# Feature tiles of the input projection: three 256-column matmuls per weight tile, or one of 512 columns and one of 256

## The chip, the cores and the metric

The kernel runs on one core of a Trainium2 chip. The metric is the device time of one execution in microseconds (us), the median of several runs. The core has five engines that matter here: TensorE (PE in the profile, with its weight loads as PEld), VectorE (DVE), ScalarE (ACT), GpSimd (POOL) and the DMA queues of SyncE (SP). Each engine works off its own instructions in the order in which they stand in the program, and waits at an instruction until what it needs is there.

## The reference

Two layers of a decoder trunk on 256 tokens with 1024 features, in float32. What is changed is the product `h @ w_in`.

```python
for l in range(DEPTH):                       # two layers
    h = rms_norm(x, norm_mix[l])
    z = h @ w_in[l]                          # 1024 x 4768, the input projection
    c_q, c_kv, k_pe, hq, hf, hi, hg, g_a, g_b = jnp.split(z, offsets, axis=-1)
    y_a = mla_mixer(c_q, c_kv, k_pe, ...) @ w_proj_a[l]        # latent attention
    y_b = hgrn2_mixer(hq, hf, hi, hg, ...) @ w_proj_b[l]       # gated recurrence
    y = sigmoid(g_a) * y_a + sigmoid(g_b) * y_b
    x = x + y @ w_out[l]
    h = rms_norm(x, norm_ffn[l])
    x = x + (silu(h @ w_gate[l]) * (h @ w_up[l])) @ w_down[l]
```

## The kernel before

**Two parts for every operand.** Each float32 operand of a large product is split into a high part and a remainder, both in the float32r format of TensorE. ScalarE writes the high part of a weight chunk (`wh`, L113), VectorE the remainder (`wl`, L115). For half of each of the chunks t3 to t6 GpSimd writes the remainder in its place (`ON_POOL`). A product is then the sum of three: high by high, high by remainder, remainder by high. `mm3` (L191) issues these three as matmuls of 256 columns (the 256 tokens), each with its own weight load. `mmw` (L205) exists too, and the two SwiGLU products use it: because the two parts of the activations lie side by side in `xx` as [8, 2, 256], one matmul of 512 columns takes both with the high weights, and a second of 256 columns adds the remainder of the weights to the first half of the PSUM bank. The bank's halves must then be added on the way out.

**Chunks and tiles.** 33 blocks of 128 output features ("tiles" below) of the input projection are computed with features on partitions and tokens as columns. `T_CHUNKS` puts one into chunk t0 and two into each of t1 to t16, and `tchunk(ci)` computes a chunk: both tiles into the two halves of one PSUM bank, eight weight tiles of 128 features deep, 24 matmuls per tile. Then one VectorE instruction per chunk (L277 or L281) multiplies the whole bank, 512 columns, by the norm's scale `rb` on its way to SBUF; for t9 to t16 a ScalarE tanh follows (L282). t0 to t2 give the attention's latents, t3 and t4 the forget gates `hf`, t5 and t6 the recurrence's queries `hq`, t7 and t8 its output gate, t9 to t16 the merge gates.

**PSUM.** The pool `acc` has two banks, for t0, t1 and t3 to t16 (t2 takes one of `hgp`) and for the two token tiles of the recurrence's values (`hia`, L313). A chunk can begin when the chunk but one before it has been read out of its bank.

**Order.** The Python code issues t0 to t2, the latents, the keys and queries of attention (L365 to L404), then t3 to t16 with steps of attention (`next(at)`) and of the recurrence (`next(rec)`) between chunks, so that TensorE has matmuls of the projection while the other engines work at softmax and recurrence. A list scheduler of the framework then sets the final order on each engine. Weights are prefetched up to two chunks ahead into five buffers for `wh` and five for `wl`, each of half a chunk, so one tile uses one buffer of each. `gates(h)` (L495 to L500) takes `hf` through exp (ScalarE), an addition (GpSimd), a reciprocal and two scalings (VectorE); `rows` (L600, L601) and `products` (L540) begin the recurrence once `hq` and the gates are there.

Of the kernel before, what the change touches and what calls it, by code (L numbers as in the profile page):

```python
# [9 lines left out]
F32 = mybir.dt.float32  # L10
# [4 lines left out]
ALU = mybir.AluOpType  # L15
# [17 lines left out]
# columns of the packed per-partition vectors  # L33
# [3 lines left out]
# weight parts whose remainders GpSimd takes, where the vector engine has most to do  # L37
# [6 lines left out]
def chunk_plan():  # L44
    """Chunks of one layer in the order of their use: (name, columns per partition)."""
    plan = [("t0", 1024)]
    plan += [(f"t{i}", 2048) for i in range(1, 3)]
    plan += [("hib", 2176), ("ukv", 2048), ("uq0", 1152), ("uq1", 1152)]
    plan += [(f"t{i}", 2048) for i in range(3, 7)]
    plan += [("hia", 2176)]  # L50
    plan += [(f"t{i}", 2048) for i in range(7, 17)]
    plan += [(f"proj{i}", 2048) for i in range(4)]
    plan += [(f"out{i}", 2048) for i in range(4)]
    plan += [(f"gu{i}", 2048) for i in range(KF)]
    plan += [(f"dn{i}", 2048) for i in range(11)]
    return plan
# [10 lines left out]
# the 33 feature tiles of w_in that are computed with features on partitions  # L67
# [12 lines left out]
def trunk(ctx: ExitStack, tc: tile.TileContext, x_in, w_in, vec_in, gqk_in, cst_in, msk_in, out):  # L80
# [44 lines left out]
    # intra-tile score matrices of the recurrence (transposed); entries above the causal  # L125
    # diagonal stay zero
# [32 lines left out]
    # lower bounds of the forget gates: lbm = 1 - lb per layer  # L159
# [22 lines left out]
    def split(hi, lo, src, scale=None):  # L182
        """hi + lo = src * scale, both parts float32r."""
        if scale is None:
            S.copy(hi, src)
            V.tensor_tensor(lo, src, hi.bitcast(F32), ALU.subtract)
        else:
            S.activation(hi, src, AF.Copy if isinstance(scale, float) else AF.Identity, scale=scale)  # L188
            V.scalar_tensor_tensor(lo, src, scale, hi.bitcast(F32), ALU.mult, ALU.subtract)  # L189
# [15 lines left out]
    def mmw(ps, items):  # L205
        """Both parts of the moving operand in one pass; ps[:, 0] + ps[:, 1] is the product."""
        n = len(items)
        for i, ((ah, al), b) in enumerate(items):
            PE.matmul(ps, ah, b, start=i == 0, stop=False)  # L209
            PE.matmul(ps[:, 0], al, b[:, 0], start=False, stop=i == n - 1)  # L210

    def token_stats(src, kt, both=False):
        """Sum of squares over features (partitions and kt tiles) per token -> PSUM [tok, TT]."""
        tot = None
        for k in range(kt):
            sq = wk.tile([P, T], F32, tag="w1", bufs=3, name="sq")
            if k % 2 or not both:
                S.activation(sq, src[:, k], AF.Square)  # L218
            else:
                V.tensor_tensor(sq, src[:, k], src[:, k], ALU.mult)  # L220
            if tot is None:
                tot = sq
            else:
                G.tensor_tensor(tot, tot, sq, ALU.add)  # L224
        ps = trp.tile([P, 512], F32, name="trp")
        for t in range(TT):
            PE.matmul(ps[:, t:t + 1], tot[:, t * P:(t + 1) * P], ones[:, 0:1], start=True, stop=True)
        return ps[:, 0:TT]

    def norm_in(l, col):  # L230
        """Split gain * x, and the norm's scale per token, [tok, TT] and broadcast over partitions."""
# [18 lines left out]
    for l in range(L):  # L250
# [11 lines left out]
        def tchunk(ci):  # L262
            W = weights(l, f"t{ci}")
            tiles = T_CHUNKS[ci]
            if ci == 2:
                ps = hgp.tile([P, 2, T], F32, name="hgp")
            else:
                ps = acc.tile([P, 2, T], F32, name="acc")
            for j in range(len(tiles)):
                o = j * KD * P  # L270
                mm3(ps[:, j], [(W(o + k * P, P), xs[k]) for k in range(KD)], late=l == 0 and ci == 0)
            n = len(tiles)
            a = tiles[0]
            rbb = bc(rb.unsqueeze(1), [P, n, T])
            for lo, hi, dst in ((0, 5, cq), (5, 9, hf), (9, 13, hq), (13, 17, sg)):
                if lo <= a < hi:
                    V.tensor_tensor(dst[:, a - lo:a - lo + n], ps[:, :n], rbb, ALU.mult)  # L277
            if a >= 17:
                m = (a - 17) // 2
                g = wk.tile([P, 2, T], F32, name="gs", bufs=2)  # L280
                V.tensor_tensor(g, ps, rbb, ALU.mult)  # L281
                S.activation(gab[:, m], g, AF.Tanh, scale=0.5)  # L282
# [4 lines left out]
        # latents: gain and split; their norms' scales come in after the next product  # L287
# [33 lines left out]
        # rotary tables with the gains; the gains of the other dimensions go to the queries  # L321
# [33 lines left out]
        def heads_T(dst, src, t, i):  # L355
            """Four heads of 128 tokens, their dimensions to partitions."""
# [63 lines left out]
        # scale of each row of scores  # L420
# [9 lines left out]
        # causal softmax and its product with the values  # L430
# [60 lines left out]
        # gates: k = (1 - lb) sigmoid(-hf), f = 1 - k  # L491
# [10 lines left out]
        # Scores by the highest bit in which two positions differ. Level h: row t (bit h set)  # L502
        # against column s in the first half of the same 2h block. q carries the decay since its
        # h block's start, k the decay to its h block's end, tot the blocks' whole decays. One set
        # of k serves levels h and 2h: for 2h, columns of the block's first h block also need the
        # decay of the second, which all rows of the second half share.
# [24 lines left out]
        def tiles(ap, h, u):  # L531
            """One head's positions with bit h set to u: [tile, block, position]."""
            return half(ap, h, u).rearrange("p (t n) c -> p t n c", t=TT)

        def products(rw, cols):
            """Scores of one head's columns k against the packed rows."""
# [15 lines left out]
        def blocks(h):  # L552
            """Levels whose columns are whole groups of 32 partitions."""
# [41 lines left out]
        def recurrence():  # L595
            # the diagonal and level 1
# [14 lines left out]
            # levels 2 and 4, levels 8 and 16  # L611
# [135 lines left out]
def _tiles(w, ks, ms):  # L747
    """[K, M] -> [128, ms, ks, 128]: the weight tiles of each output tile side by side."""
# [3 lines left out]
def _pack(inp):  # L752
# [36 lines left out]
    # constants of the shapes  # L789
# [37 lines left out]
```

## Time and profile before

| | us |
|---|---|
| median of 3 runs (787.41 to 787.87) | 787.68 |
| span of the profiled execution, first to last instruction | 785.7 |
| between the two (what lies around the span) | 2.0 |
| PE busy | 769.1 (98%) |
| PEld busy | 716.8 (91%) |
| DVE busy | 614.7 (78%) |
| ACT busy | 414.8 (53%) |
| POOL busy | 277.7 (35%) |

The busy time of PE is not a measure of how fast its matmuls follow each other: they are pipelined, and a matmul's row lasts longer than the distance to the next. That distance is read from the starts in the timeline. A plain float32 matmul (transposes, scores, the recurrence) stands as two records in the trace in most lines. The shares over the whole span mix stages: the input projection with attention and recurrence lies at 20 to 167 us in the first layer and 400 to 551 us in the second, the SwiGLU behind each.

### The profile page before, as it was taken

How to read it: one execution, taken by the hardware profiler on the slowest of the kernel's cores; microseconds unless marked ns; L12 is line 12 of the kernel's file. 1: busy time of each engine (PE TensorE's matmuls, PEld its weight loads, DVE VectorE, ACT ScalarE, POOL GpSimd, SP SyncE). 2: the span in 40 equal slices, each digit the busy share in tenths (PEclk: the TensorE clock that was granted, in tenths of full speed). 3: DMA queues.
4: the chain of work that ended last, by engine and by line, in shares of the span. 5: the costliest groups of instructions: out<-in, count | busy, mean ns of one | idle time of the engine just before them, and what ended most of it. 6: DMA issues, size and time to landing. Idle time of an engine off the chain costs nothing.

```text
span 785.7 us, 13803 instructions
## 1 busy us (share of the span) xinstructions
PE 769.1 (98%) x5376; PEld 716.8 (91%) x5376; DVE 614.7 (78%) x958; ACT 414.8 (53%) x744; POOL 277.7 (35%) x296
## 2 busy tenths in 40 slices
PE   5999999999999999999999999999999999999998
PEld 4999999999988888888899999999999888888887
DVE  7799986658979888886668898856687988888652
ACT  5665754444655656554447557444354655655430
POOL 5696422003234343421037823311223334444000
PEclk9999999999999999999999999999999999999999
DMA  7743334425554545455534443334454564545630
GB/s 244 261 166 126 143 112 158 161 108 216 172 204 161 210 166 212 166 211 205 193 122 161 165 161 108 137 134 161 161 181 149 208 214 168 209 168 208 226 131 20
DMA packets 20658, 133.27 MB, mean 170 GB/s; under 512 B 2417, under 2 KB 3569, under 8 KB 5361
## 3 DMA queue, kind: packets, MB, share of 16 engines
q1 hardware_dynamic: 20592, 132.39, 47.3%
q8 instruction: 42, 0.69, 0.3%
q14 instruction: 24, 0.19, 0.1%
HBM read 131.33 MB, written 1.05 MB: 168 GB/s over the span
## 4 chain that ended last, share of the span: by engine, by line
PE 82%; DVE 12%; issue 3%; POOL 1%; ACT 1%; DMA 1%; SPq 0%; DVEq 0%; POOLq 0%; ACTq 0%
PE acc L209 15%; PE acc L210 8%; PE acc L202 8%; PE acc L203 8%; PE acc L201 8%; PE prj L209 5%; PE hgp L209 5%; PE trp L209 5%; DVE wl L115 3%; PE trp L210 3%; PE hgp L210 3%; PE prj L210 3%; PE hgp L540 2%; DVE hf L498 1%; PE prj L201 1%
## 5 line engine op out<-in xcount | busy, mean ns | idle before, releaser
L115 DVE TENSOR_TENSOR wl<-st,wh 128x1024 fp32r<-128x1024 f32 (+3 forms) x241 | 327.1, 1359 | 68.2 <-ACT wh L113 67.3
L113 ACT CAST wh<-st 128x1024 fp32r<-128x1024 f32 (+2 forms) x250 | 257.8, 1035 | 178.3 <-PE acc L202 88.5
L201 PE MATMUL acc<-xx,wh 128*128 128x256 f32 x488 | 141.1, 289 | 0.0
L203 PE MATMUL acc<-xx,wl 128*128 128x256 f32 x488 | 139.2, 286 | 0.0
L202 PE MATMUL acc<-xx,wh 128*128 128x256 f32 x488 | 139.0, 285 | 0.0
L209 PE MATMUL acc<-ff,wh 128*128 128x512 f32 x352 | 122.4, 391 | 0.0
L210 PE MATMUL acc<-ff,wl 128*128 128x256 f32 x352 | 98.9, 282 | 0.0
L202 PEld LDWEIGHTS acc<-xx,wh 128*128 128x128 f32 x488 | 93.3, 191 | 0.3
L201 PEld LDWEIGHTS acc<-xx,wh 128*128 128x128 f32 x488 | 93.3, 191 | 0.3
L203 PEld LDWEIGHTS acc<-xx,wl 128*128 128x128 f32 x488 | 93.2, 191 | 0.1
L722 POOL TENSOR_TENSOR g<-g,rb 128x256 f32<-128x256 f32 x44 | 37.2, 846 | 135.3 <-DVE g L721 123.0
L209 PEld LDWEIGHTS acc<-ff,wh 128*128 128x128 f32 x352 | 66.1, 188 | 14.2 <-DVE ff L189 0.4
L727 POOL TENSOR_TENSOR hd<-th,g 128x256 f32<-128x256 f32 x44 | 66.1, 1503 | 7.4 <-DVE th L725 4.5
L188 ACT ACTIVATE ff<-hd 128x256 fp32r<-128x256 f32 x44 | 18.4, 418 | 94.4 <-POOL hd L727 94.4
L224 POOL TENSOR_TENSOR sq<-sq 128x256 f32<-128x256 f32 x34 | 33.9, 996 | 96.7 <-ACT sq L218 58.8
L210 PEld LDWEIGHTS acc<-ff,wl 128*128 128x128 f32 x352 | 66.5, 189 | 0.1
L209 PE MATMUL prj<-xx,wh 128*128 128x512 f32 x176 | 62.4, 396 | 0.0
L209 PE MATMUL acc<-xx,wh 128*128 128x512 f32 x176 | 62.3, 394 | 0.0
L209 PE MATMUL hgp<-xx,wh 128*128 128x512 f32 x176 | 62.1, 394 | 0.0
L209 PE MATMUL trp<-xx,wh 128*128 128x512 f32 x176 | 62.0, 393 | 0.0
L210 PE MATMUL acc<-xx,wl 128*128 128x256 f32 x176 | 49.0, 279 | 0.0
L210 PE MATMUL hgp<-xx,wl 128*128 128x256 f32 x176 | 48.8, 277 | 0.0
(238 smaller groups left out, 1765.4 us busy)
## 6 DMA issues: line engine op xcount, KB each, us to landing
st<-in_w_dram SPq DMA_DIRECT2D x115, 1024.0 KB, 4.7
st<-in_w_dram SPq DMA_DIRECT2D x4, 1088.0 KB, 4.9
st<-in_w_dram SPq DMA_DIRECT2D x4, 576.0 KB, 3.5
st<-in_w_dram SPq DMA_DIRECT2D x4, 512.0 KB, 5.1
xT<-in_x_dram SPq DMA_DIRECT2D x4, 256.0 KB, 4.8
out_dram<-xT SPq DMA_DIRECT2D x8, 128.0 KB, 1.9
mst<-in_msk_dram SPq DMA_DIRECT2D x1, 288.0 KB, 7.2
cst<-in_cst_dram SPq DMA_DIRECT2D x1, 260.0 KB, 7.4
```

Of the source, the lines that this page charges most:

```text
L113: S.copy(wh[:, :n_], st[:, c:c + n_])
L115: eng.tensor_tensor(wl[:, :n_], st[:, c:c + n_], wh[:, :n_].bitcast(F32), ALU.subtract)
L188: S.activation(hi, src, AF.Copy if isinstance(scale, float) else AF.Identity, scale=scale)
L201: PE.matmul(ps, ah, bh, start=i == 0, stop=False)
L202: PE.matmul(ps, ah, bl, start=False, stop=False)
L203: PE.matmul(ps, al, bh, start=False, stop=i == n - 1)
L209: PE.matmul(ps, ah, b, start=i == 0, stop=False)
L210: PE.matmul(ps[:, 0], al, b[:, 0], start=False, stop=i == n - 1)
L224: G.tensor_tensor(tot, tot, sq, ALU.add)
L540: PE.matmul(ps[:, t * 192:(t + 1) * 192], kk[:, hd, t * P:(t + 1) * P], rt[:, t], start=True, stop=True)
L722: (V, G)[j].tensor_tensor(g[:, j], g[:, j], rb, ALU.mult)
L727: G.tensor_tensor(hd, th, g[:, 1], ALU.mult)
```

## The change

From t3 on each tile gets a bank of `acc` of its own and is computed with `mmw`: eight pairs of a 512-column and a 256-column matmul in place of 24 of 256 columns. Per tile, ScalarE copies the bank's second half to `g`, and VectorE adds the first half to it. Per chunk, GpSimd multiplies both tiles by `rb` into the destination, where VectorE did it out of PSUM before. t0 to t2 are left as they were. The rest of the change is comments that are taken out; the lines of the changed kernel that follow `tchunk` stand ten lines lower.

```diff
         def tchunk(ci):
             W = weights(l, f"t{ci}")
             tiles = T_CHUNKS[ci]
-            if ci == 2:
-                ps = hgp.tile([P, 2, T], F32, name="hgp")
-            else:
-                ps = acc.tile([P, 2, T], F32, name="acc")
-            for j in range(len(tiles)):
-                o = j * KD * P
-                mm3(ps[:, j], [(W(o + k * P, P), xs[k]) for k in range(KD)], late=l == 0 and ci == 0)
             n = len(tiles)
             a = tiles[0]
             rbb = bc(rb.unsqueeze(1), [P, n, T])
-            for lo, hi, dst in ((0, 5, cq), (5, 9, hf), (9, 13, hq), (13, 17, sg)):
+            dst = None
+            for lo, hi, d in ((0, 5, cq), (5, 9, hf), (9, 13, hq), (13, 17, sg)):
                 if lo <= a < hi:
-                    V.tensor_tensor(dst[:, a - lo:a - lo + n], ps[:, :n], rbb, ALU.mult)
-            if a >= 17:
-                m = (a - 17) // 2
-                g = wk.tile([P, 2, T], F32, name="gs", bufs=2)
-                V.tensor_tensor(g, ps, rbb, ALU.mult)
-                S.activation(gab[:, m], g, AF.Tanh, scale=0.5)
+                    dst = d[:, a - lo:a - lo + n]
+            if ci < 3:
...
+                return
+
+            g = wk.tile([P, 2, T], F32, name="gs", bufs=2)
+            for j in range(n):
+                o = j * KD * P
+                ps = acc.tile([P, 2, T], F32, name="acc")
+                mmw(ps, [(W(o + k * P, P), xx[:, k]) for k in range(KD)])
+                S.copy(g[:, j], ps[:, 1])
+                V.tensor_tensor(g[:, j], g[:, j], ps[:, 0], ALU.add)
+            G.tensor_tensor(g if dst is None else dst, g, rbb, ALU.mult)
+            if dst is None:
+                S.activation(gab[:, (a - 17) // 2], g, AF.Tanh, scale=0.5)
```

The scheduler moves other work with it. Three places of the first layer follow; the numbers in names count allocations, so equal numbers in the two kernels are not the same tile.

On PE, before, where chunk t5 (acc_988) ends and t6 (acc_1075) begins:

```order
L203 MATMUL acc_988<-xx_141,wl_880 128x256
L201 MATMUL acc_988<-xx_141,wh_879 128x256
L202 MATMUL acc_988<-xx_141,wh_879 128x256
L203 MATMUL acc_988<-xx_141,wl_880 128x256
L201 MATMUL acc_1075<-xx_141,wh_980 128x256
L202 MATMUL acc_1075<-xx_141,wh_980 128x256
L203 MATMUL acc_1075<-xx_141,wl_981 128x256
```

On PE, now, the same place (acc_988 is the second tile of t5, acc_1046 the first of t6; trp_848 takes transposes of the softmax, prj_924 scores):

```order
L209 MATMUL acc_988<-xx_141,wh_869 128x512
L210 MATMUL acc_988<-xx_141,wl_870 128x256
L465 MATMUL trp_848<-cst_108,pr_766 128x128 x4
L449 MATMUL prj_924<-kT_466,qT_465 128x256 x2
L209 MATMUL acc_1046<-xx_141,wh_960 128x512
L210 MATMUL acc_1046<-xx_141,wl_961 128x256
L209 MATMUL acc_1046<-xx_141,wh_960 128x512
```

Four transposes of the softmax and two matmuls of scores, which stood singly inside t6, now stand in one piece between the two tiles.

On DVE, before, from a weight remainder behind t4's reading out to the reading out of t5's bank (acc_988):

```order
L115 TENSOR_TENSOR wl_1068<-st_1065,wh_1067 128x1088
L442 TENSOR_REDUCE mx_762<-prj_756 128x4
L428 TENSOR_SCALAR nsc_738<-sc_737 128x8
L500 TENSOR_SCALAR ff_751<-hf_199 128x256
L440 TENSOR_TENSOR prj_842<-prj_842,cst_108 128x512
L498 RECIPROCAL hf_199<-hf_199 128x256
L444 TENSOR_TENSOR nb_764<-mx_762,nsc_738 128x4
L498 RECIPROCAL hf_199<-hf_199 128x256
L115 TENSOR_TENSOR wl_1072<-st_1065,wh_1071 128x1088
L442 TENSOR_REDUCE mx_848<-prj_842 128x4
L277 TENSOR_TENSOR hq_200<-acc_988,rb_193 128x512
```

On DVE, now, from the reading out of t4's second tile (acc_893) to that of t5's first (acc_969):

```order
L289 TENSOR_TENSOR gs_873<-gs_873,acc_893 128x256
L450 TENSOR_TENSOR prj_756<-prj_756,cst_108 128x512
L452 TENSOR_REDUCE mx_762<-prj_756 128x4
L508 RECIPROCAL hf_199<-hf_199 128x256
L454 TENSOR_TENSOR nb_764<-mx_762,nsc_738 128x4
L508 RECIPROCAL hf_199<-hf_199 128x256
L115 TENSOR_TENSOR wl_1042<-st_1035,wh_1041 128x1088
L450 TENSOR_TENSOR prj_832<-prj_832,cst_108 128x512
L289 TENSOR_TENSOR gs_968<-gs_968,acc_969 128x256
```

The reciprocals of the gates of t3 now stand between the additions that free the banks of two neighbouring tiles; a bank is freed tile by tile.

On POOL, before, from the weight remainder of t5 on:

```order
L115 TENSOR_TENSOR wl_880<-st_873,wh_879 128x1024
L497 TENSOR_SCALAR hf_199<-hf_199 128x256
L403 TENSOR_TENSOR qh_710<-qh_710,sw_714 128x4x32
L497 TENSOR_SCALAR hf_199<-hf_199 128x256
L157 TENSOR_TENSOR sc_737<-mq_744,cst_108 128x8
L115 TENSOR_TENSOR wl_985<-st_978,wh_984 128x1024
L497 TENSOR_SCALAR hf_199<-hf_199 128x256 x2
```

On POOL, now, from the same remainder on:

```order
L115 TENSOR_TENSOR wl_870<-st_863,wh_869 128x1024
L290 TENSOR_TENSOR hf_199<-gs_782,rb_193 128x512
L157 TENSOR_TENSOR sc_737<-mq_744,cst_108 128x8
L413 TENSOR_TENSOR qh_710<-qh_710,sw_714 128x4x32
L115 TENSOR_TENSOR wl_965<-st_958,wh_964 128x1024
L507 TENSOR_SCALAR hf_199<-hf_199 128x256 x2
L290 TENSOR_TENSOR hf_199<-gs_873,rb_193 128x512
```

The new multiplication stands ahead of the power that makes the scales of the scores, and the additions of the gates come behind the next weight remainder.

## Rows read from the trace of the kernel before

**Rows 1.** Page, part 1: busy us, share of the span and instructions by engine.

```profile
PE 769.1 (98%) x5376; PEld 716.8 (91%) x5376; DVE 614.7 (78%) x958; ACT 414.8 (53%) x744; POOL 277.7 (35%) x296
```

**Rows 2.** Windows: stretch, busy us (count) of PE, PEld, DVE, ACT, POOL; clock, DMA.

```profile
42.00:90.00 48.00, 47.66 (x369) 46.61 (x368) 47.90 (x88) 29.63 (x62) 32.31 (x27) 1.00 0.44 155
90.00:167.00 77.00, 77.00 (x669) 76.52 (x668) 56.50 (x97) 39.20 (x71) 16.69 (x20) 1.00 0.38 138
428.00:476.00 48.00, 48.00 (x379) 47.31 (x378) 45.93 (x84) 30.24 (x66) 29.66 (x25) 1.00 0.43 153
```

**Rows 3.** Timeline, PE, inside chunk t10: start us, us, engine, line, operation.

```profile
119.78 0.28 PE L203 MATMUL acc<-xx,wl 128*128 128x256 f32 x1
...
122.06 0.28 PE L201 MATMUL acc<-xx,wh 128*128 128x256 f32 x1
```

**Rows 4.** Timeline, PE, gate and up product, where `mmw` runs.

```profile
299.78 0.39 PE L209 MATMUL hgp<-xx,wh 128*128 128x512 f32 x1
...
303.94 0.39 PE L209 MATMUL acc<-xx,wh 128*128 128x512 f32 x1
```

**Rows 5.** Timeline, PE, the merge's projection, three 256-column matmuls in the quickest stretch.

```profile
180.00 0.28 PE L201 MATMUL acc<-ah,wh 128*128 128x256 f32 x1
...
180.35 0.28 PE L201 MATMUL acc<-ah,wh 128*128 128x256 f32 x1
```

**Rows 6.** Timeline, PE, transposes inside t4, the matmuls behind, and t5's first matmul.

```profile
59.93 0.60 PE L359 MATMUL trp<-cst,qh 128*96 128x128 f32 x4
60.29 0.36 PE L201 MATMUL acc<-xx,wh 128*128 128x256 f32 x1
60.49 0.28 PE L202 MATMUL acc<-xx,wh 128*128 128x256 f32 x1
...
62.77 0.28 PE L201 MATMUL acc<-xx,wh 128*128 128x256 f32 x1
```

**Rows 7.** Groups by form: line, engine, operation xcount | busy us, mean ns | idle before.

```profile
L277 DVE TENSOR_TENSOR hf<-acc,rb 128x512 f32<-128x512 f32 x4 | 2.7, 678 | 0.0
L721 DVE TENSOR_TENSOR g<-g,acc 128x256 f32<-128x256 f32 x22 | 9.0, 407 | 0.0
L720 ACT COPY g<-acc 128x256 f32<-128x256 f32 x22 | 8.0, 365 | 0.0
L520 POOL TENSOR_TENSOR hf<-hf,ff 128x512 f32<-128x512 f32 x8 | 10.8, 1353 | 60.5 <-DVE hf L520 45.7 <-PE hgp L540 7.5 <-PE hgp L562 7.3
```

**Rows 8.** Timeline, DVE, first layer, 57 to 82 us: the banks' readings and what lies between.

```profile
57.35 0.68 DVE L277 TENSOR_TENSOR hf<-acc,rb 128x512 f32<-128x512 f32 x1
...
62.39 3.35 DVE L498 RECIPROCAL hf<-hf 128x256 f32<-128x256 f32 x2
...
70.26 0.67 DVE L442 TENSOR_REDUCE mx<-prj 128x4 f32<-128x512 f32 x1
...
76.80 0.67 DVE L277 TENSOR_TENSOR hq<-acc,rb 128x512 f32<-128x512 f32 x1
```

**Rows 9.** Timeline, PE, the first matmul of `hia`, into t5's bank.

```profile
77.53 0.39 PE L201 MATMUL acc<-wh,xx 128*128 128x272 f32 x1
```

**Rows 10.** Timeline, second layer, DVE: a small scaling beside POOL's weight remainder.

```profile
440.98 2.33 DVE L427 TENSOR_SCALAR sc<-sc,rc 128x8 f32<-128x8 f32 x1
```

**Rows 11.** Timeline, POOL, the same stretch.

```profile
440.88 2.39 POOL L115 TENSOR_TENSOR wl<-st,wh 128x1024 fp32r<-128x1024 f32 x1
```

**Rows 12.** Timeline, DVE, SwiGLU: two weight remainders and the additions behind them.

```profile
262.06 1.22 DVE L115 TENSOR_TENSOR wl<-st,wh 128x1024 fp32r<-128x1024 f32 x1 [0.18 <-ACT wh L113]
...
263.87 1.76 DVE L115 TENSOR_TENSOR wl<-st,wh 128x1024 fp32r<-128x1024 f32 x1
265.55 0.41 DVE L721 TENSOR_TENSOR g<-g,acc 128x256 f32<-128x256 f32 x1
```

**Rows 13.** Timeline, ACT, SwiGLU: the cast ahead of that slower remainder.

```profile
262.51 1.04 ACT L113 CAST wh<-st 128x1024 fp32r<-128x1024 f32 x1
```

**Rows 14.** Timeline, POOL, beside the slower of the two remainders.

```profile
264.62 1.60 POOL L727 TENSOR_TENSOR hd<-th,g 128x256 f32<-128x256 f32 x1
```

More of the change, by code (lines that the diff above doesn't have):

```diff
@@ L274, in tchunk @@
             rbb = bc(rb.unsqueeze(1), [P, n, T])
-            for lo, hi, dst in ((0, 5, cq), (5, 9, hf), (9, 13, hq), (13, 17, sg)):
+            dst = None
+            for lo, hi, d in ((0, 5, cq), (5, 9, hf), (9, 13, hq), (13, 17, sg)):
                 if lo <= a < hi:
-                    V.tensor_tensor(dst[:, a - lo:a - lo + n], ps[:, :n], rbb, ALU.mult)
-            if a >= 17:
-                m = (a - 17) // 2
-                g = wk.tile([P, 2, T], F32, name="gs", bufs=2)
-                V.tensor_tensor(g, ps, rbb, ALU.mult)
-                S.activation(gab[:, m], g, AF.Tanh, scale=0.5)
+                    dst = d[:, a - lo:a - lo + n]
+            if ci < 3:
+                if ci == 2:
+                    ps = hgp.tile([P, 2, T], F32, name="hgp")
+                else:
+                    ps = acc.tile([P, 2, T], F32, name="acc")
+                for j in range(n):
+                    o = j * KD * P
+                    mm3(ps[:, j], [(W(o + k * P, P), xs[k]) for k in range(KD)], late=l == 0 and ci == 0)
+                V.tensor_tensor(dst, ps[:, :n], rbb, ALU.mult)
+                return
+            g = wk.tile([P, 2, T], F32, name="gs", bufs=2)
+            for j in range(n):
+                o = j * KD * P
+                ps = acc.tile([P, 2, T], F32, name="acc")
+                mmw(ps, [(W(o + k * P, P), xx[:, k]) for k in range(KD)])
[4 more added lines that the diff above has]
+                S.activation(gab[:, (a - 17) // 2], g, AF.Tanh, scale=0.5)
         for ci in range(3):
```

## Prediction

> **What bounds the kernel now.** The page's first part [rows 1] says TensorE 98%, VectorE 78%, so I read TensorE first, then asked by windows where another engine fills up. In the first layer's stretch from 42 to 90 us VectorE is busy 47.90 of 48 us, in the second layer's from 428 to 476 us 45.93 of 48; from 90 to 167 us it has 56.5 of 77 [rows 2]. So two stages matter here. In the early one (keys and queries, then chunks t3 to t6) both engines are full, in the later one (t7 to t16) TensorE alone. That VectorE already sets the pace in the early one is seen at one place: t5's bank is read out from 76.80 for 0.67, to 77.47 [rows 8], and the next user of that bank starts at 77.53 [rows 9]. TensorE itself is busy 47.66 of the 48 us there and 77.00 of 77 behind, so what its stream gains is time, unless a new wait eats it.
>
> **The change part by part.** All sums are made against the profiled span of 785.7 us; the 2.0 us between it and the median of 787.68 I carry over unchanged.
>
> *The stream.* 14 chunks of 2 tiles, 2 layers, 8 weight tiles deep: 448 triples of 256-column matmuls become 448 pairs (512 and 256 columns). The columns are the same, 768; what goes is 448 matmuls with their weight loads. In t10 19 matmuls start within 122.06 - 119.78 = 2.28 us [rows 3]: 0.120 each, 0.360 a triple. In the gate and up product 12 pairs take 303.94 - 299.78 = 4.16 us [rows 4]: 0.347 a pair. The saving is 0.0133, times 448 gives 6.0 us. From below: the quickest triple of the trace takes 0.350 [rows 5], which leaves 0.003 a pair, 1.5 us. I take 6.0, because rows 3 are the very matmuls that go, and in rows 4 the pairs read the same layout `xx`.
>
> Here a page has a rule of its own. The Trainium skill ("TensorE: Matmul & The Clock Gate", Back-to-back issue gap) gives a warm matmul of N columns N/2.4 plus 2.5 ns. By it a triple is an estimated 0.328 us and a pair 0.325, and the saving would be 1.1 us in place of 6.0. The trace doesn't agree in size: 0.360 and 0.347, so that a matmul costs more beside its columns than the rule says.
>
> *Breaks in the stream.* Where TensorE changes from plain float32 back to the split operands, the second matmul follows after 60.49 - 60.29 = 0.20, not 0.12 [rows 6]. In the program's order such breaks fall from 79 to 71, since the softmax's transposes no longer stand singly inside chunks. 8 times 0.08 is 0.6 us.
>
> *Work added elsewhere.* ScalarE: 56 copies of 0.365 = 20 us. VectorE: 56 additions of 0.407 less 28 multiplications of 0.678 = 3.8 us more. GpSimd: 28 multiplications of 512 columns; a like one takes 1.353 [rows 7], 38 us. From 90 us on all three have room [rows 2] and I cost this at nothing. No DMA is added or moved past another queue; bytes and prefetch depth stay.
>
> *The banks, early stage.* A bank was freed per chunk; a chunk could start when the one before the last was read out, so TensorE had about 5.7 us of cover. Now it is freed per tile, and the cover is one tile, 8 x 0.347 = 2.8 us, plus what stands between tiles. VectorE, being full, can be followed by adding durations in the new order.
> - t3's second addition stands where t3's bank was read before (57.35, [rows 8]): done at 57.8. Behind it come the instructions that filled the time up to 62.39 before, with one reduction now behind the scaling that waits for GpSimd instead of ahead of it, 0.3 later: t4's first tile is added at 62.39 + 0.3 + 0.41 = 63.1. TensorE began t5 at 62.77 [rows 6] and now gets there about 0.4 earlier (four tiles of 0.11). t5's first tile needs that bank: wait 0.8.
> - t5's first addition stands behind the addition of t4's second tile, two masks and a reduction of about 0.67 each, two reciprocals (3.35 for two), two weight remainders of about 1.25 and small scalings [rows 8, 12], some 8.9 us; GpSimd's part of the gates comes 0.7 late for the first reciprocal, behind its multiplication and a weight remainder. 63.1 + 9.6 = 72.7. TensorE has two tiles (5.6) and, between them, two sets of transposes (0.36 each, [rows 6]) and two of scores, for which I allow an estimated 0.8 each; the second transposes also wait some 0.9, because the exponentials they read start behind the first reciprocal. It arrives at 72.2: wait 0.5.
> - t5's second addition comes another reciprocal, reduction, remainder, mask and scalings later, 77.4; TensorE, one tile and one set of value products on, is there at 76.3: wait 1.1.
>
> That is 0.8 + 0.9 + 0.5 + 1.1 = 3.3 us. Queued behind those waiting matmuls are the scores of the next heads and the recurrence's first products; behind the late additions stands GpSimd's multiplication into `hq`, 1.35 us that the recurrence's rows now wait for. I add 0.2 a layer for that.
>
> In the second layer the same order has a worse place: t3's second addition now stands behind the small scaling that took 2.33 us, from 440.98 [rows 10], and behind two remainders and the queries' products, at an estimated 445.6 to 447.3, by whether the scaling is held again; TensorE needs that bank at about 443.9. Middle: 2.5 us, the later additions fitting into the cover but for 0.4. Bounds: 1.2 (the scaling slips past) and 4.4.
>
> Together: 3.5 + 2.9 = 6.4 us lost; between 2.5 (half of the waits of the first layer do not come, the low end in the second) and 11.
>
> *The banks, later stage.* Reading out a tile is now cast, remainder, addition one behind the other, because the order puts the weight cast and remainder that refill the buffer of this very tile ahead of its copy and addition: 1.04 [rows 13], 1.22 and 0.41 [rows 12], 2.7 us against a cover of 2.8. In nearly all places transposes or recurrence matmuls stand between two tiles as well. I cost it at 0.2 us in all; the bound is in the rivals.
>
> Sum: -6.0 - 0.6 + 6.4 + 0.2 = 0.0. I forecast the median as it is, 787.7 us: no change that can be told. By the page's rule above the sum would be 4.9 us more, near 792.6.
>
> **The rivals.**
> - *The waits do not come (faster).* The additions are short, and if VectorE reaches them even 1 us earlier than I add up, three of the four waits in the first layer vanish. For it: the scheduler put every addition ahead of work that nobody on TensorE waits for. Against: 47.90 of 48 us busy [rows 2]. With 2.5 us of waits left: 787.7 - 6.6 + 2.5 = 783.6.
> - *GpSimd holds up VectorE (slower).* The trace has a 128x8 scaling on VectorE that takes 2.33 us from 440.98 [rows 10], while GpSimd's remainder runs from 440.88 for 2.39 [rows 11]: it ends when GpSimd does. And a remainder of 1.22 on VectorE takes 1.76 beside a multiplication on GpSimd [rows 12, 14]. Eight of the new multiplications fall into the early stages, where VectorE has nothing to spare. At 0.54 each that is 4.3 us more on the engine that TensorE waits for: 787.7 + 4.3 = 792.0, and it decides as soon as the multiplications of t3 to t6 overlap VectorE's remainders or scalings. Against it: GpSimd runs weight remainders there already, and part of the overlap exists. The Trainium skill ("GPSIMD Engine Reference", Key points) states that GpSimd shares its SBUF interfaces with VectorE and contends with instructions of two SBUF inputs; the rows just named agree.
> - *The later banks ring (slower).* If the remainder is the 1.76 one, cast, remainder and addition take 3.2 us, 0.4 more than the cover; if half of the 40 later tiles lose 0.3 to that, 6 us: 793.7.
> - *The stream gains little (slower).* With 1.5 us in place of 6.0 [rows 5]: 792.2. Rows 4 speak against it.
>
> **How the numbers follow.** A difference of 0.2% (1.6 us) is about what a measurement of this kernel can tell from none. No change 0.37 (own range 786.1 to 789.3), the waits do not come 0.36, GpSimd holds up VectorE 0.16, later banks 0.06, little gain 0.05. So faster 0.36, same 0.37, slower 0.27. The range of 8 in 10 goes from 782.5, below the faster case by a us, to 792, which leaves out the later ring and the worst of the early waits.
>
> **What would show it.** In the new profile 4928 matmul records in place of 5376; pairs of 0.347 us by their starts in t3 to t16, in place of 0.360 (wrong if 0.350 or more). Holes on TensorE of 0.5 to 1.1 us ahead of the tiles of t5 and t6 in the first layer and of about 2 us ahead of t4's second in the second layer, each ended by an addition at L289 (wrong if below 0.3, or of 3 us). No hole ahead of tiles from t7 on. Additions of 0.41 and GpSimd multiplications of 1.0 to 1.5 us; scalings and remainders that last longer beside them would speak for the second rival. If the later chunks show regular holes behind the remainders, the third holds.

## The result, and the profile after

The changed kernel takes 795.54 us (median of 4 runs, 795.45 to 795.59) against 787.77 of the kernel before in the same session: ratio 1.0096, 95% interval 1.0083 to 1.0108. It is slower by 7.8 us where no change was forecast, and outside the range. Its profiled span is 793.8 us.

The page's first part, in the columns of [rows 1], and the windows of [rows 2]:

```profile
PE 770.1 (97%) x4928; PEld 694.3 (87%) x4928; DVE 624.8 (79%) x986; ACT 432.3 (54%) x800; POOL 318.7 (40%) x324
```

```profile
42.00:90.00 48.00, 43.41 (x264) 37.90 (x263) 47.44 (x85) 29.00 (x63) 34.58 (x29) 1.00 0.46 155
90.00:167.00 77.00, 76.70 (x520) 68.74 (x520) 60.46 (x110) 45.16 (x93) 32.11 (x32) 1.00 0.37 124
428.00:476.00 48.00, 43.14 (x257) 38.51 (x257) 44.05 (x83) 29.75 (x65) 33.66 (x29) 0.96 0.40 133
```

The matmul records are down to 4928, as they should be. Over the whole span the shares hardly differ. By stage they do: in 42 to 90 us TensorE now stands idle for 4.6 us (48.00 - 43.41) where it was 0.3 [rows 2], in 428 to 476 us for 4.9 where it was 0, and there the mean clock is 0.96. VectorE is as full as before in the first and not quite in the second. In 90 to 167 us TensorE loses 0.3.

The idle time of TensorE, from its timeline; in brackets the idle time ahead of an instruction and what ended it. First the first layer, then the second:

```profile
64.80 0.50 PE L209 MATMUL acc<-xx,wh 128*128 128x512 f32 x1 [1.64 <-DVE gs L289]
69.51 0.50 PE L209 MATMUL acc<-xx,wh 128*128 128x512 f32 x1 [0.29 <-DVE gs L289]
73.11 1.65 PE L465 MATMUL trp<-cst,pr 128*128 128x128 f32 x4 [0.52 <-ACT pr L459]
76.34 0.47 PE L209 MATMUL acc<-xx,wh 128*128 128x512 f32 x1 [0.71 <-DVE gs L289]
81.13 0.47 PE L209 MATMUL acc<-xx,wh 128*128 128x512 f32 x1 [0.89 <-DVE gs L289]
...
451.06 0.50 PE L209 MATMUL acc<-xx,wh 128*128 128x512 f32 x1 [2.79 <-DVE gs L289]
...
461.14 1.10 PE L471 MATMUL trp<-av,pT 128*128 128x64 f32 x8 [0.75 <-ACT pT L467]
462.97 0.50 PE L209 MATMUL acc<-xx,wh 128*128 128x512 f32 x1 [0.72 <-DVE gs L289]
```

All but two of these holes end with an addition (L289) that frees a tile's bank: t5's two tiles and t6's two in the first layer, t4's second and t5's second in the second layer. The second layer has one more hole, 0.60 at 456.99, which ends with an exponential on ScalarE. At 73.11 four transposes of the softmax take 1.65 us where four of the queries' took 0.60 [rows 6]: each waits for its own exponential.

To set the terms side by side I took, for every matmul, the distance from its start to the next start, less the median distance of that kind of matmul over both kernels; what is over the median I call waiting, although it also holds the cost of a lower clock. In us, the kernel before and after: 40 to 100 us 0.9 and 7.2; 420 to 480 us 0.1 and 7.5; 100 to 180 us 0.2 and 1.8; 480 to 560 us 0.8 and 1.9; the two merges (180 to 220 and 560 to 600 us) together 2.2 and -1.2. The waiting grows by 13.0, and the medians' sum falls by 5.4 from fewer matmuls; 7.6, and the first matmul started 0.5 later in this execution: 8.1, the difference of the spans. The early stage alone costs 13.6 us more, where the forecast had 6.4.

What VectorE and GpSimd do in the first layer ahead of the first two holes (VectorE, then GpSimd; start, us):

```profile
58.04 2.47 DVE L437 TENSOR_SCALAR sc<-sc,rc 128x8 f32<-128x8 f32 x1
60.54 1.23 DVE L438 TENSOR_SCALAR nsc<-sc 128x8 f32<-128x8 f32 x1
...
64.34 0.41 DVE L289 TENSOR_TENSOR gs<-gs,acc 128x256 f32<-128x256 f32 x1
65.17 0.42 DVE L437 TENSOR_SCALAR sc<-sc,rc 128x8 f32<-128x8 f32 x1 [0.42 <-POOL sc L157]
65.62 2.31 DVE L438 TENSOR_SCALAR nsc<-sc 128x8 f32<-128x8 f32 x1
67.84 1.28 DVE L115 TENSOR_TENSOR wl<-st,wh 128x1088 fp32r<-128x1088 f32 x1
69.05 0.41 DVE L289 TENSOR_TENSOR gs<-gs,acc 128x256 f32<-128x256 f32 x1
```

```profile
58.07 2.41 POOL L115 TENSOR_TENSOR wl<-st,wh 128x1024 fp32r<-128x1024 f32 x1
60.45 1.30 POOL L290 TENSOR_TENSOR hf<-gs,rb 128x512 f32<-128x512 f32 x1
...
65.52 2.38 POOL L115 TENSOR_TENSOR wl<-st,wh 128x1024 fp32r<-128x1024 f32 x1
```

Three scalings of eight columns take 2.47, 1.23 and 2.31 us, and each ends when a GpSimd instruction ends: 60.51 and 60.48, 61.77 and 61.75, 67.93 and 67.90. The second of them ends with the new multiplication (L290). This is the mechanism of [rows 10, 11], several times over. The groups of the two lines, before (L427, L428) and after (L437, L438); xcount | busy us, mean ns:

```profile
L427 DVE TENSOR_SCALAR sc<-sc,rc 128x8 f32<-128x8 f32 x4 | 4.6, 1158 | 2.0 <-POOL sc L157 2.0
L428 DVE TENSOR_SCALAR nsc<-sc 128x8 f32<-128x8 f32 x4 | 0.7, 176 | 0.0
```

```profile
L438 DVE TENSOR_SCALAR nsc<-sc 128x8 f32<-128x8 f32 x4 | 7.7, 1926 | 0.1
L437 DVE TENSOR_SCALAR sc<-sc,rc 128x8 f32<-128x8 f32 x4 | 4.6, 1144 | 2.1 <-POOL sc L157 2.1
```

The eight took 5.3 us and take 12.3. The second of each pair, 0.16 to 0.22 before, now falls where GpSimd is busy with a weight remainder or a multiplication: directly behind the first in the first layer, behind a remainder or a reduction in the second (445.82 and 454.41).

In the second layer the clock comes on top. Windows of 461 to 469 us, in the columns of [rows 2]; the granted clock stands third from the right:

```profile
461.00:463.00 2.00, 1.14 (x9) 1.00 (x9) 2.00 (x5) 1.35 (x3) 0.00 (x1) 1.00 0.00 0
...
464.00:466.00 2.00, 2.00 (x8) 1.71 (x7) 2.00 (x5) 1.50 (x7) 1.01 (x2) 0.50 0.00 0
...
467.00:469.00 2.00, 2.00 (x14) 1.80 (x13) 2.00 (x6) 1.45 (x3) 0.67 (x1) 1.00 0.65 131
```

After the two holes at 461 and 463 us the granted clock is 0.50 (1.2 in place of 2.4 GHz). With 0.69 in 463 to 464 us and 0.61 in 466 to 467, that is some 3.4 us at 0.50, of which half, 1.7 us, is lost. Clock 0.96 over the 48 us of the window above agrees: 0.04 x 48 = 1.9, from a rounded clock.

### The profile page after: what moved, and what is told of

The parts are those of the page before. It is cut to its first block, busy times and chain, and to the rows that moved or that the text cites. A ratio compares the mean times of both kernels' runs of the same rounds, so it can differ in the third digit from the quotient of the medians.

```text
span 793.8 us, 12993 instructions
## 1 busy us (share of the span) xinstructions
PE 770.1 (97%) x4928; PEld 694.3 (87%) x4928; DVE 624.8 (79%) x986; ACT 432.3 (54%) x800; POOL 318.7 (40%) x324
## 4 chain that ended last, share of the span: by engine, by line
PE 82%; DVE 11%; POOL 4%; ACT 1%; issue 1%; DMA 1%; SPq 0%; POOLq 0%; ACTq 0%
PE acc L209 24%; PE acc L210 12%; PE prj L209 5%; PE hgp L209 5%; PE trp L209 5%; PE acc L202 4%; PE acc L203 4%; PE acc L201 4%; DVE wl L115 3%; PE hgp L210 3%; PE trp L210 3%; PE prj L210 3%; PE hgp L550 1%; PE prj L202 1%; PE prj L201 1%; PE prj L203 1%
## 5 line engine op out<-in xcount | busy, mean ns | idle before, releaser
L209 PE MATMUL acc<-xx,wh 128*128 128x512 f32 x624 | 227.7, 404 | 7.8 <-DVE gs L289 7.7
L210 PE MATMUL acc<-xx,wl 128*128 128x256 f32 x624 | 176.3, 282 | 0.0
L209 PEld LDWEIGHTS acc<-xx,wh 128*128 128x128 f32 x624 | 118.0, 189 | 35.6 <-DVE gs L289 7.8
L210 PEld LDWEIGHTS acc<-xx,wl 128*128 128x128 f32 x624 | 118.5, 190 | 0.2
L210 PE MATMUL trp<-xx,wl 128*128 128x256 f32 x176 | 48.8, 277 | 0.0
L210 PE MATMUL prj<-xx,wl 128*128 128x256 f32 x176 | 48.8, 277 | 0.0
L290 POOL TENSOR_TENSOR gs<-gs,rb 128x512 f32<-128x512 f32 x16 | 21.9, 1368 | 63.9 <-DVE gs L289 63.9
L189 DVE SCALAR_TENSOR_TENSOR ff<-hd,ff 128x256 fp32r<-128x256 f32 x44 | 20.8, 473 | 27.8 <-ACT ff L188 27.8
```

The source lines that it names most:

```text
L290: G.tensor_tensor(g if dst is None else dst, g, rbb, ALU.mult)
```

## The experiments

Times are medians, each with the ratio to the kernel before in the same session and its 95% interval (before: 787.7 to 788.1). All are edits of the changed kernel unless told.

**Which chunks: late and early.** The two halves of the change.

```diff
-            if ci < 3:
+            if ci < 7:                 # late: t3 to t6 as in the kernel before
-            if ci < 3:
+            if ci < 3 or ci > 6:       # early: t7 to t16 as in the kernel before
```

Early also puts the multiplication of t7 to t16 back on VectorE.

> The pairs from t7 on only; t3 to t6 as before (three matmuls, one bank per chunk, VectorE multiplies). Theory (the loss lies in the banks of t3 to t6, where 13.3 us of waiting came in; t7 to t16 lost 2.6): 320 pairs at 0.010 give 3.2, less 2.6, and the hole of 1.2 us in each layer's merge stays away or comes back: 784 to 788 us, faster than before or equal. Rival (read-outs of tile banks are late everywhere, so that the later stage loses too): 790 or more.

> Pairs and tile banks in t3 to t6 only; t7 to t16 as before. The complement of late. If the two halves add up: 787.8 + (795.5 - 783.2) = 800.1 us, with the holes of 1.2 us in the merge back in both layers, since they went only in kernels whose later chunks are pairs. If the early loss depends on what the later chunks do: 795 or less.

Late: 783.16 us, 0.9942 (0.9928 to 0.9955). Early: 798.24 us, 1.0132 (1.0118 to 1.0145). The loss sits in t3 to t6, and late is faster than either kernel. The halves add up to 787.9 - 4.8 + 10.2 = 793.3 against 795.5, within 2.2 us of additive. By the sums of starts late's gain is 3.8 of shorter stream and 3.2 of the merge, less 1.7 of waits in the later chunks and 0.4 in the early ones. TensorE's waits for VectorE (in all, times, longest), early and then late:

```profile
PE acc L209 <- DVE gs L294: 5.2, 5, 2.8
...
PE acc L202 <- DVE yl L189: 2.1, 2, 1.0
```

```profile
PE acc L209 <- DVE gs L289: 0.3, 1, 0.3
```

**Where the scalings stand: sc_act, and late_sc as its control** (late_sc has late's edit too; `rcq` takes SCALE in once, earlier).

```diff
-            V.tensor_scalar(sc[:, t], sc[:, t], rcq[:, t:t + 1], SCALE, ALU.mult, ALU.mult)
-            V.tensor_scalar(nsc[:, t], sc[:, t], -1.0, None, ALU.mult)
+            S.activation(sc[:, t], sc[:, t], AF.Identity, scale=rcq[:, t:t + 1])
+            S.activation(nsc[:, t], sc[:, t], AF.Identity, scale=-1.0)
```

> As after, but the two small scalings of the scores' scales (128x8, two per token tile) stand on ScalarE instead of VectorE; all else keeps its place in VectorE's queue. In after they take 2.47, 1.23 and 2.31 us in the first layer and 2.34, 1.27 and 1.82 us in the second, each ending when a GpSimd instruction ends. Theory (VectorE, held by GpSimd in these scalings, frees the tile banks late): 5 to 8 us come back, 787 to 790 us. Rival (the sheer amount of VectorE's work between two additions sets the banks): at most 2 us, 793 to 795.

> As late (pairs from t7 on only), with the scalings of the scores on ScalarE. Control for the run above: where chunk banks cover VectorE's lateness, taking the held scalings away should bring nothing: 782.5 to 783.5 us against 783.2 of late. If it brings 2 us or more, the gain above is not about the tile banks.

sc_act: 791.46 us, 1.0046 (1.0034 to 1.0059), 4.1 us less than after; below the 5 to 8 expected, above the rival's 2. late_sc: 782.56, 0.9933 (0.9919 to 0.9946), 0.6 less than late: where a bank holds a whole chunk the same edit brings almost nothing. As a control it is weak, since in late's order only two of the eight scalings are held, as before (5.6 us in all, against 12.3 in after); the kernel banks below is a better one. In the first layer's early stage of sc_act (42 to 100 us) TensorE's waits are:

```profile
PE trp L467 <- ACT pr L461: 1.5, 1, 1.5
PE acc L209 <- DVE gs L289: 0.4, 1, 0.4
```

and the scalings' groups, on ScalarE:

```profile
L439 ACT ACTIVATE sc<-sc,rc 128x8 f32<-128x8 f32 x4 | 1.2, 302 | 0.7 <-POOL sc L157 0.6
L440 ACT ACTIVATE nsc<-sc 128x8 f32<-128x8 f32 x4 | 0.9, 214 | 0.1
```

The four bank waits of the first layer (3.5 us) are one of 0.4. A wait for the softmax's exponentials, 0.5 in after, grew to 1.5, and behind it the granted clock falls, in the first layer where it had been 1.00 in after:

```profile
60.00:80.00 20.00, 17.74 (x93) 14.54 (x91) 16.73 (x27) 9.32 (x25) 13.40 (x11) 0.83 0.44 158
```

A mean of 0.83 over 20 us is 0.50 for 6.8 us, 3.4 us lost. So by the sums of starts the early stage of the first layer gained only 0.8 us, and that of the second 2.9, of which 1.7 is the clock, which stays at 1.00 there. One more reason why it is less than expected: the small operation ahead of GpSimd's power (`mq`), which stayed on VectorE, now meets GpSimd's weight remainder in each layer and takes 1.88 and 2.19 us.

**Is it the form of the instruction: sc_tt.** Same engine, same places, two tiles in place of a tile and a scalar (`neg` is a tile of -1; `rcq` takes SCALE in as in sc_act).

```diff
+            V.tensor_tensor(sc[:, t], sc[:, t], bc(rcq[:, t:t + 1], [P, NH]), ALU.mult)
+            V.tensor_tensor(nsc[:, t], sc[:, t], neg, ALU.mult)
```

> As after, the two scalings of the scores' scales still on VectorE and in the same places, but as multiplications of two SBUF tiles instead of a tile by a scalar. If only the one-tile form is held until GpSimd's instruction ends: the eight take 0.1 to 0.4 us each in place of 12.3 in all, and 4 us come back as with ScalarE, 790 to 792 us. If any VectorE instruction that reads SBUF twice is held as well: durations of 1.2 to 2.4 us as in after, and 795 us.

794.26 us, 1.0083 (1.0069 to 1.0097), 1.3 less than after, which the intervals do not separate. The groups, and one of the instructions with GpSimd's beside it:

```profile
L442 DVE TENSOR_TENSOR nsc<-sc,neg 128x8 f32<-128x8 f32 x4 | 8.7, 2186 | 0.1
L441 DVE TENSOR_TENSOR sc<-sc,rc 128x8 f32<-128x8 f32 x4 | 2.2, 560 | 2.1 <-POOL sc L159 2.1
```

```profile
64.66 2.31 DVE L442 TENSOR_TENSOR nsc<-sc,neg 128x8 f32<-128x8 f32 x1
```

```profile
64.56 2.38 POOL L115 TENSOR_TENSOR wl<-st,wh 128x1024 fp32r<-128x1024 f32 x1
```

10.9 us in place of 12.3, the hold ends at 66.97, GpSimd at 66.94: of these two forms both are held, and the neighbour decides. The Trainium skill ("SBUF — State Buffer", SBUF: two separate sides) states that VectorE and GpSimd share a port pair that one of them locks for a whole instruction, and counts VectorE instructions with two SBUF inputs among those that need it; this trace agrees for the product of two tiles, with 2.31 us beside 2.38, and the traces above show the same of a tile by a scalar.

**GpSimd's multiplication: mulv_early and dummy.** mulv_early puts it on VectorE in t3 to t6; dummy adds it, unused, to the kernel before, for the same chunks.

```diff
-            G.tensor_tensor(g if dst is None else dst, g, rbb, ALU.mult)
+            (V if ci < 7 else G).tensor_tensor(g if dst is None else dst, g, rbb, ALU.mult)
```

```diff
                     V.tensor_tensor(dst[:, a - lo:a - lo + n], ps[:, :n], rbb, ALU.mult)
+                    if 3 <= ci < 7:
+                        gd = wk.tile([P, 2, T], F32, tag="gs", name="gd", bufs=2)
+                        G.tensor_tensor(gd, dst[:, a - lo:a - lo + n], rbb, ALU.mult)
```

> As after, but the multiplication by rb of t3 to t6 stands on VectorE instead of GpSimd (8 of about 0.6 us more on VectorE in the early stages). Theory that GpSimd's multiplications hold VectorE's small scalings up (1.07 and 1.14 us in the first layer) and push GpSimd's weight remainders beside others (2.15): about 3 to 4 us come back, 790 to 793 us. Rival (VectorE has too much to do per bank, holds or not): the 5 us of added work come on top, 798 to 801 us.

> The kernel before with 8 more GpSimd multiplications of 128x512 (one for each of t3 to t6 in each layer, of the tile just read out, into a buffer that nobody reads). Tells what GpSimd's multiplications cost without the tile banks. Theory that they hold VectorE up by themselves: 4 us or more, 792 us. Rival (holds decide only because a tile's bank gives half the cover that a chunk's gave): 787.5 to 789.

mulv_early: 792.74 us, 1.0069 (1.0056 to 1.0081), 2.8 less than after. dummy: 790.42, 1.0032 (1.0020 to 1.0045), 2.6 more than before. The scalings' groups in mulv_early:

```profile
L437 DVE TENSOR_SCALAR sc<-sc,rc 128x8 f32<-128x8 f32 x4 | 5.6, 1409 | 1.0 <-POOL sc L157 1.0
L438 DVE TENSOR_SCALAR nsc<-sc 128x8 f32<-128x8 f32 x4 | 3.0, 742 | 0.0
```

8.6 us in place of 12.3, although VectorE got 8 multiplications more: so VectorE's lateness is not a matter of its own work alone. The time itself says less: by the sums of starts 1.5 us of the gain lie in the early stages and 1.5 in the later chunks, which the edit does not touch. In dummy the scalings take 7.7 us in place of 5.3, and the time goes up by 2.6, between the two expectations: GpSimd's multiplications cost something with chunk banks as well. The scalings that are still long in mulv_early (2.46, 2.35 and 2.34 us) stand beside GpSimd's weight remainders.

**More banks: banks, banks_sc, best34.** The second tile of t3 to t6 takes a bank of `hgp`; banks_sc has sc_act's edit too; best34 has both, but keeps three matmuls in t5 and t6.

```diff
-                ps = acc.tile([P, 2, T], F32, name="acc")
+                if ci < 7 and j:
+                    ps = hgp.tile([P, 2, T], F32, name="hgp")
+                else:
+                    ps = acc.tile([P, 2, T], F32, name="acc")
```

> As after, but the second tile of t3 to t6 takes a bank of hgp, so that four banks turn round in the early stage. Theory (TensorE waits for banks that VectorE frees late): most of the 13.3 us goes, 783 to 786 us. Rival (VectorE's lateness itself reaches TensorE through softmax and gates, whatever banks there are): 790 to 795 us, with the waits now ahead of the softmax's transposes.

> Both: four banks in t3 to t6 and the scalings on ScalarE. If bank waits and VectorE's lateness are all of the early loss, the early stage returns to about the wait of before and the pairs of t3 to t6 gain 1.3 us over late: 782 to 784 us. Rival (the softmax's and the recurrence's chain through GpSimd's multiplication of hq is the next bound, as the 1.4 and 2.6 us waits for L614 in banks hint): 785 to 787.

> Pairs in t3, t4 (with four banks) and t7 to t16, three matmuls in t5 and t6, the scalings on ScalarE. The waits that banks_sc kept lie at t5 and t6 in the first layer; 64 more pairs than late_sc at 0.010: 782.0 us if t3 and t4 add no waits, 783 to 785 if they do.

banks: 788.71 us, 1.0005 (0.9996 to 1.0014), 6.8 less than after. banks_sc: 783.94, 0.9951 (0.9939 to 0.9964), 11.6 less. best34: 782.26, 0.9934 (0.9921 to 0.9946), level with late_sc. TensorE's waits in the early stages of banks, first and second layer:

```profile
PE hgp L553 <- POOL rows L614: 1.4, 1, 1.4
PE acc L209 <- DVE gs L292: 0.3, 1, 0.3
```

```profile
PE hgp L553 <- POOL rows L614: 2.6, 1, 2.6
PE trp L468 <- ACT pr L462: 1.2, 1, 1.2
```

With four banks the bank waits are gone to 0.3, although the eight scalings are held nearly as long as in after (11.6 us): with cover enough VectorE's lateness no longer reaches TensorE through the banks. What is late next is GpSimd with the recurrence's rows (L614), which stand behind its multiplication into `hq`; that was the rival's part of the expectation, and banks lies between the two. The gains of the two edits (4.1 and 6.8) add up to nearly what both bring (11.6), but only over the whole. Waiting in the two early stages by the sums of starts, us:

| | first layer | second layer |
|---|---|---|
| after | 7.2 | 7.5 |
| sc_act | 6.5 | 4.6 |
| banks | 3.0 | 6.3 |
| banks_sc | 2.9 | 0.3 |

In the first layer the banks bring nearly all; in the second either edit alone leaves more than half, and both together leave almost nothing. So these are not two costs that add up, but two sides of the same waits: VectorE's additions come late, and two banks give a tile too little cover. Of the 6.3 us in banks some 1.7 are the granted clock, which falls to 0.50 for 3.4 us behind the two waits of the second layer. What that is worth the eleven executions of banks tell: the five with a mean clock of 0.999 took 787.4 to 787.7 us, the six with 0.997 or 0.998 took 788.7 to 789.4. banks_sc came out at 783.9 with 2.9 us of waits left in the first layer's early stage, 2.1 more than late_sc has; best34, which takes t5 and t6 out again, at the 782 that was expected.

**The scales on GpSimd: sc_pool, late_scpool, banks_scpool.** All three small operations beside GpSimd's power; the same three kernels as above otherwise.

```diff
-            V.tensor_scalar(mq, ssq[:, t], rcq2[:, t:t + 1], EPS, ALU.mult, ALU.add)
+            G.tensor_scalar(mq, ssq[:, t], rcq2[:, t:t + 1], EPS, ALU.mult, ALU.add)
             power(sc[:, t], mq)
+            G.tensor_scalar(sc[:, t], sc[:, t], rcq[:, t:t + 1], SCALE, ALU.mult, ALU.mult)
+            G.tensor_scalar(nsc[:, t], sc[:, t], -1.0, None, ALU.mult)
```

> As after, but the scores' scales are made on GpSimd altogether (three small operations of 128x8 around its power, two sets per layer): none of them can be held by a GpSimd instruction any more, and none crosses engines; in the run with ScalarE one of the three stayed on VectorE and took 1.88 us in the first layer. Theory (held scalings on VectorE make the banks late): at least what ScalarE's version brought (791.5), 788 to 791 us. Rival (GpSimd's queue, with its late multiplications for the gates, now sets the early stage): 792 to 796.

> As late (pairs from t7 on only), with the scores' scales on GpSimd. Chunk banks cover VectorE's lateness, so 782 to 783.5 us against 782.6 with ScalarE; if GpSimd's queue matters, 784 or more.

> Pairs from t3 on, four banks in t3 to t6, the scores' scales on GpSimd. With ScalarE it was 783.9, 2.1 us of it waits of the first layer's early stage beyond those of late. If the scale that stayed on VectorE caused those: 781.5 to 783. If they come from GpSimd's multiplication ahead of the recurrence's rows: 784 to 786.

792.21 us (1.0060, 1.0046 to 1.0074), 786.32 (0.9986, 0.9977 to 0.9995) and 787.45 (0.9993, 0.9985 to 1.0002): 0.8 (within the intervals), 3.8 and 3.5 us more than with ScalarE. No scaling can be held on VectorE any more, and it does not pay. In late_scpool TensorE waits instead for the softmax and for the queries, which stand behind the scales in GpSimd's queue:

```profile
PE trp L465 <- ACT pr L459: 2.0, 2, 1.2
PE trp L369 <- POOL qh L413: 1.2, 1, 1.2
```

So these runs say that GpSimd's queue is a limit of its own in the early stage, and that an edit that was expected to be neutral moves the time by up to 4 us through that queue.

**The stream alone: three.** The bank and the way out of after, but from the second k-step on three matmuls of 256 columns.

```diff
-                mmw(ps, [(W(o + k * P, P), xx[:, k]) for k in range(KD)])
+                for k in range(KD):
+                    wh, wl = W(o + k * P, P)
+                    if k == 0:
+                        PE.matmul(ps, wh, xx[:, k], start=True, stop=False)
+                    else:
+                        PE.matmul(ps[:, 0], wh, xx[:, k, 0], start=False, stop=False)
+                        PE.matmul(ps[:, 1], wh, xx[:, k, 1], start=False, stop=False)
+                    PE.matmul(ps[:, 0], wl, xx[:, k, 0], start=False, stop=k == KD - 1)
```

> As after, with its banks and its way out, but in 7 of 8 k-steps the 512-column matmul is two of 256 columns again. Tells what the stream alone is worth. If a pair saves 0.010 us against a triple: 392 steps, of which 112 lie in t3 to t6 where TensorE waits for banks anyway: 2.8 to 3.9 us slower than after, 798.3 to 799.4 us. If the stream gains nothing: 795.5.

803.23 us, 1.0194 (1.0180 to 1.0208), 7.7 more than after, where 2.8 to 3.9 was expected. Two triples, from 150.39 to 151.11, are 0.72 us, 0.360 each:

```profile
150.39 0.28 PE L292 MATMUL acc<-xx,wh 128*128 128x256 f32 x1
...
151.11 0.28 PE L292 MATMUL acc<-xx,wh 128*128 128x256 f32 x1
```

So the 0.010 a pair is there, 3.9 us over 392 steps. By the sums of starts 2.5 more are the merge's holes, which are back in this run; 1.3 us stay open. The clock is a likely part of them: it is 0.50 for 6.8 us of the first layer's early stage here (a mean of 0.83 in 60 to 70 and in 70 to 80 us), where after has 3.4 us of it in the second layer, 1.7 us less lost.

**The later multiplication: late_sc_mulv.** late_sc with the multiplication of t7 to t16 on VectorE.

> As late with the scalings on ScalarE, but the multiplication by rb of t7 to t16 is on VectorE instead of GpSimd. If GpSimd holds VectorE up in the later stage too, the waits there (0.9 and 1.9 us in the two layers) shrink: 781 to 782 us. If VectorE has room there and the holds do not reach TensorE: 782.5; if the added 20 multiplications of about 0.6 us make the tile banks late: 784 or more.

```diff
-            G.tensor_tensor(g if dst is None else dst, g, rbb, ALU.mult)
+            V.tensor_tensor(g if dst is None else dst, g, rbb, ALU.mult)
```

784.74 us, 0.9965 (0.9953 to 0.9978), 2.2 more than late_sc. No tile bank is late, though; what came back is one wait, as in the kernel before:

```profile
PE acc L202 <- DVE yl L189: 2.1, 2, 1.0
```

In each layer's merge TensorE waits for a remainder (`yl`) that stands in VectorE's queue behind a weight remainder. The wait is there in the kernel before, dummy, early, three and late_sc_mulv, and not in the others. Nothing of the change touches those lines, and VectorE's order alone does not decide: in after too a `yl` (198.62) stands behind a weight remainder (from 196.93 for 1.77), and TensorE has other matmuls until it comes. The waits are in the kernels whose t7 to t16 are not pairs, in three, and in late_sc_mulv; what in the later chunks moves them is not shown, since no run changed the merge's order alone.

## Why the prediction was wrong

*The stream: right in kind, a quarter too large.* Pairs in t7 to t16 of after follow at 0.347 to 0.350, for instance seven in 2.43 us (0.347 each):

```profile
147.32 0.40 PE L209 MATMUL acc<-xx,wh 128*128 128x512 f32 x1
...
149.75 0.39 PE L209 MATMUL acc<-xx,wh 128*128 128x512 f32 x1
```

The median over 100 to 167 us is 0.350, so that a pair saves 0.010, 4.5 us in all where 6.0 was forecast; by the prediction's own sign (wrong if 0.350 or more) the term is at the edge. With the breaks the medians' sum fell by 5.4 where 6.6 was forecast. The 1.1 us by the Trainium skill's rule ("TensorE: Matmul & The Clock Gate", Back-to-back issue gap), which the prediction weighed there, was too small; the section gives that rule for an isolated matmul, and these stand in a stream.

*Work added elsewhere: the durations were right.*

```profile
L290 POOL TENSOR_TENSOR gs<-gs,rb 128x512 f32<-128x512 f32 x16 | 21.9, 1368 | 63.9 <-DVE gs L289 63.9
L288 ACT COPY gs<-acc 128x256 f32<-128x256 f32 x56 | 20.6, 368 | 0.5 <-PE acc L210 0.4
L289 DVE TENSOR_TENSOR gs<-gs,acc 128x256 f32<-128x256 f32 x56 | 23.0, 412 | 0.0
```

*The banks, early stage: the step that failed.* It read VectorE's lateness off by adding durations of the trace before in the new order. The places came out: holes ahead of t5's and t6's tiles, the softmax's transposes, t4's second tile in the second layer. The durations did not stay what they were. A scaling of 0.2 us takes up to 2.5 beside a GpSimd instruction, and in the new order six of the eight are held there instead of two, 7.0 us more on the engine that was full. The prediction had the mechanism as a rival, but priced it at 0.54 for each new multiplication and looked for it at these multiplications; four of the six holds end with weight remainders, which GpSimd did before too. In the sum by starts the bank waits are 4.2 and 3.8 us in the two layers (forecast 2.4 and 2.9); the waits of transposes and value products for ScalarE 2.3 and 1.7 (forecast 0.9 and none); the lower clock in the second layer 1.7 (not foreseen). So of the 7.2 us beyond the forecast the banks themselves are some 2.7, the waits for ScalarE 3.1 and the clock 1.7. By the order of events each is a step behind the one before it: late banks delay the scores, late scores the exponentials, and the clock falls behind the holes. That sc_act and banks give 4.1 and 6.8 back is measured, and that both leave 3.2 of the 14.7 us of early waiting; that the clock's 1.7 belongs to the holes is read from the order of events (banks_sc, without those holes, has a mean clock of 1.00) and was not tested by itself.

*The banks, later stage: too small, if these are the banks.* Waiting there grew by 2.6 us where 0.2 stood; the third rival had 6. Only one wait in each layer, 0.3 and 0.4 us, is put down to a bank by the profile; the rest is spread over small gaps, none above 0.2 us, and its cause stays open.

*Not foreseen: the merge.* 3.4 us were gained in a stage that the diff does not touch: 2.7 around the two holes that are gone, the rest by matmuls that follow a little closer.

The sum as measured: -5.4 stream, +13.6 early, +2.6 later, -3.4 merge, 7.4 of 7.8 us. The forecast of 0.0 was -6.6 + 6.4 + 0.2.

## What to carry to other kernels

A duration from a trace holds for its neighbours in that trace: before adding durations in a new order, look what GpSimd does beside VectorE at that moment, and price a small scaling on VectorE beside a weight remainder or multiplication on GpSimd at up to the length of the latter, as six of the eight came out here. When a buffer is cut from two tiles to one, the cover is cut as well; do it only where the engine that empties it has room, as here from the seventh chunk on, where the same edit is 0.6% faster. And before a gain is credited to an edit, look whether an untouched stage moved: two thirds of that gain (3.2 of 4.8 us) came from the merge.

## What the runs showed of the hardware

- A scaling of 8 columns on VectorE takes up to 2.5 us beside a weight remainder or multiplication on GpSimd and ends within 0.03 us of it, as a tile by a scalar or as a product of two tiles. Not every neighbour does this: beside GpSimd's addition of a scalar (L497 of the kernel before, from 447.93 to 448.80) the scaling of 447.99 took 0.36 us and ended 0.45 us ahead of it. Nor is every VectorE instruction held: the reciprocal of 70.70 in after takes 1.74 us beside a multiplication on GpSimd, and 1.73 at 73.41 in the kernel before with GpSimd idle. GpSimd is held in turn: a weight remainder that takes 2.38 alone takes 3.43 where VectorE's remainder began 0.02 us ahead of it (second layer of after; VectorE, then GpSimd):

```profile
444.68 1.21 DVE L115 TENSOR_TENSOR wl<-st,wh 128x1024 fp32r<-128x1024 f32 x1
```

```profile
444.70 3.43 POOL L115 TENSOR_TENSOR wl<-st,wh 128x1024 fp32r<-128x1024 f32 x1
```

- TensorE's granted clock, 1.00 throughout the kernel before, fell to 0.50 for some 3.4 us in after, behind two idle times of 0.7 us that followed one of 2.8 us ten us earlier, and for 6.8 us in sc_act, behind one of 1.55 us.
